# More slots for gathered rows while the mixers run, and four PSUM banks by turns for the dense U tiles

## The chip, the cores and the metric

The kernel runs on one core of a Trainium2 chip. A time is the device time of one execution in microseconds (us). The core has four engines that compute, each with its own queue of instructions in a fixed order: TensorE (PE, matmuls), VectorE (DVE), ScalarE (ACT) and GpSimd (POOL). SyncE (SP) only issues DMAs, and ACT and POOL issue DMAs too. Lower is better.

## The reference

One layer on 512 tokens of width 1024: three token mixers, merged by gates, then a mixture of 16384 one-neuron experts, from which each token takes 16 for each of 8 heads.

```python
h = rmsnorm(x, norm1_g)
z = h @ w_in                       # q, k, v and gates of the three mixers
merged = g0 * (fox(z) @ w_fox_o) + g1 * (window(z) @ w_swa_o) + g2 * (memory(z, mem) @ w_mem_o)
x = x + merged @ w_out

h = rmsnorm(x, norm2_g)
q = h @ w_q                        # 8 heads x 2 halves x 128
s1, s2 = q[..0..] @ keys1, q[..1..] @ keys2
v1, i1 = top_k(s1, 16); v2, i2 = top_k(s2, 16)
cand = v1[:, None] + v2[None, :]   # 256 a head
sv, si = top_k(cand, 16)
experts = i1[si // 16] * 128 + i2[si % 16]
a = einsum('cd,ced->ce', h, u[experts])
act = gelu(a) * softmax(sv)
x = x + einsum('ce,ced->cd', act, v[experts])
```

So a token needs 128 rows of u and 128 rows of v, 1024 numbers each.

## The kernel before

The 512 tokens are four blocks of 128. Two ways of computing the experts are mixed. Blocks 0 and 1 go by **rows**: for each of the 128 chosen experts POOL issues an indirect DMA that fetches one row of u (later of v) for each of the 128 tokens, a tile of 128x1024 (L876); DVE multiplies it with the tokens and sums (L891, for u), or adds it, scaled, to the result (L898 in the mixers, L904 later, for v). That makes 512 rows. A few are done by POOL and ACT instead ("apart"). Blocks 2 and 3 go **dense**: U tile k (128 experts) is multiplied with all 256 tokens, then weighted by a matrix of gates that is zero where an expert was not chosen, and the product with V tile k is summed over all 128 k.

The order of the work:

- `mixers(0)` for block 0, then the search and choice of its experts beside the begin of `mixers(1)` for blocks 1 to 3.
- `mixers(1)`: matmuls on PE in three terms of split operands (L145 to L147), with weights loaded by SP (L113, tile `raw`), cast by ACT (L119) and split by DVE (L131). Beside it the generator `beside()` does the rows of block 0, one `step()` at a time, at a priority `LATER` below the mixers; so a row fills what the mixers leave of DVE. `EARLY_ROWS` rows are done by the end of the mixers. (`fox` is one of the mixers; `fox(1, 1)` its second half of heads for blocks 1 to 3.)
- The search of blocks 1 to 3: PE multiplies with w_pq (L113 loads) and with the keys (`keys`, loaded at L744, used at L760), ACT copies the scores (L763), DVE finds the best (L717 to L721). One row is done per `PER_ROW` of the search's cost. The first `FIRST_U` = 4 dense U tiles lie here.
- The cover: from here DVE, POOL and PE keep the order in which the code is written. PE does `COVER` dense U tiles one after the other (L1040, 8 matmuls in the program; ACT's gelu at L1042 empties the PSUM bank), while DVE chooses the experts and does a row per `AMONG`. The softmax's `ex` (L790) is ACT's, and waits for DVE (L814).
- The spreading: 64 steps build the gate matrices (DVE L1100 and L1118, ACT L1103 and L1121, PE L1115), with the remaining `DURING` U tiles up to `LAG` between the steps' matmuls on PE, and rows on DVE.
- The main loop over the 128 V tiles: V tile k, the U tiles that are left (split in two, L1027 and L1029) and the remaining rows, evenly spread.

A row lies in one of five buffers of tag `row` (`ROWS_IN`), and `step()` issues gathers up to `AHEAD` = 4 rows ahead of the one that it finishes. The U tiles in PSUM use the two banks of tag `mm`; the spreading's matmuls use the two of tag `sc`. The two buffers of tag `v`, and one, named `ownlo` after the change, belong to the mixers: `ownlo` holds the low half of block 0's normalised tokens, `v` the values that `fox` reads.

What sets the order in the mixers and the search is a scheduler: it places instructions by priority and by its own estimate of times. From the cover on it is the code.

Of the kernel before, what the change touches and what calls it, by code (L numbers as in the profile page):

```python
# [1 line left out]

# [24 lines left out]
DENSE = (2, 3)  # L27
ND = len(DENSE)
TD = 128 * ND
FIRST_U, COVER, DURING, AFTER = 4, 28, 25, 0  # L30
PRE_U = 13
KEPT = FIRST_U + COVER
SPILT = (128 - KEPT) // 3
AMONG, UNWEIGHED = 1.0, 14
LAG = FIRST_U + COVER + DURING + AFTER
# [15 lines left out]
UNREAD = 36  # L51
LATER = 400
PACE = {"search": 20.0, "choose": 8.0, "rows": 3.5}
EARLY_ROWS, PER_ROW, APART, NO_APART = 176, 3.4, 4, 94.0


@with_exitstack
def tile_block(ctx: ExitStack, tc: tile.TileContext, t: dict, out: bass.AP):
# [188 lines left out]
    for hf in range(2):  # L247
        squares(xg[:, 0, hf * 512:(hf + 1) * 512], xsum[:, 0, hf:hf + 1])
    nc.sync.dma_start(cst[:, 1:], t["c_mats"][:, 1:])
    hT = [chunks(by_k(x)) for x in (ep.tile([128, D], F32R, tag="own", name="own"),  # L250
                                    pp.tile([128, D], F32R, name="ownlo", bufs=1))]
    norm_t([xg[:, 0]], xsum, g1, *hT, tags=("tp", "sc", "tp", "sc", "tg", "acc", "mm", "tp"))

    identb = consts.tile([128, 128], BF16, name="identb")
# [374 lines left out]
    def mixers(g, hT):  # L629

        nb = len(GROUPS[g])
        skvf(g, hT)
        oT = new_oT(g)
        qT = fox_qkv(g, 0, hT)
        if g == 0:
            memory()
            biases()
        fox(g, 0, qT, oT)
        qT = fox_qkv(g, 1, hT)
        fox(g, 1, qT, oT)  # L640
        merged = wide(f"mg{g}", nb)
        gs = gates(g, 0, hT)
        qT = window_q(g, hT)
        branch(g, 0, merged, oT, gs)
        oT = new_oT(g)
        window(g, qT, oT)
        gs = gates(g, 1, hT)
        qT = memory_q(g, hT)
        branch(g, 1, merged, oT, gs)
        oT = new_oT(g)  # L650
        recall(g, qT, oT)
        gs = gates(g, 2, hT)
        if g == 0:
            get_x()
        branch(g, 2, merged, oT, gs)

        mT = [by_k(ep.tile([128, D], F32, tag="own", name="own"))] if nb == 1 else pair(nb)
        if nb == 1:
            for q in range(2):
                ps = bank("tp")  # L660
                for i in range(4):
                    PE.transpose(ps[:, i * 128:(i + 1) * 128], merged[:, (4 * q + i) * 128:(4 * q + i + 1) * 128], ident)
                ps, dst = ps.rearrange("p (k s) -> p k s", k=4), slice(4 * q, 4 * q + 4)
                A.activation(mT[0][:, dst], ps, AF.Copy, scale=0.5)
        else:
            for ct, src in enumerate(chunks(by_k(merged))):
                A.activation(mT[0][:, ct], src, AF.Copy, scale=0.5)
                V.scalar_tensor_tensor(mT[1][:, ct], src, 0.5, mT[0][:, ct].bitcast(F32),  # L668
                                       op0=OP.mult, op1=OP.subtract)
        mT = [chunks(x) for x in mT]  # L670
        x1, sums = by_token(wide(f"mg{g}", nb)), new_sums(4)
        for c in range(4):
            xs = [new_g(256) for _ in range(nb)]
            cols = slice(c * 256, c * 256 + 256)
            for lb, b in enumerate(GROUPS[g]):
                nc.sync.dma_start(xs[lb], t["x"][b * 128:(b + 1) * 128, cols])

            def use(b, ps):
                V.tensor_add(x1[:, b, cols], xs[b], ps)
                squares(x1[:, b, cols], sums[:, b, c:c + 1])  # L680

            if nb == 1:
                gemm_plain(mT[0], t["w_out"][c], 256, use, load_raw)
            else:
                gemm_nat(mT, t["w_out"][c], 256, nb, use)
        return x1, sums
# [173 lines left out]


    JOBS = [(b, tab, j) for b in (0, 1) for tab in "uv" for j in range(NJ)]
    known, issued, done, ahead, flying, rpool = [2 * NJ], [0], [0], [AHEAD], {}, []
    begun_v = set()

    def step(apart=False):

        while issued[0] < min(known[0], done[0] + ahead[0] + 1):
            n = issued[0]
            issued[0] += 1  # L870
            b, tab, j = JOBS[n]
            if ahead[0] > AHEAD and n % (ROWS_IN + MORE) >= ROWS_IN:
                r = wp.tile([128, WSLOT], F32, tag="raw", name="row")[:, :D]
            else:
                r = rpool[0].tile([128, D], F32, tag="row", name="row", bufs=ROWS_IN)
            G.indirect_dma_start(out=r, out_offset=None, in_=t["peer_" + tab],  # L876
                                 in_offset=bass.IndirectOffsetOnAxis(ap=eidx[b][:, j:j + 1], axis=0))
            flying[n] = r
        n = done[0]
        done[0] += 1  # L880
        b, tab, j = JOBS[n]
        r, c = flying.pop(n), slice(j, j + 1)
        if tab == "u" and b and j == 0:
            A.copy(two[0], h2n[b])
        if tab == "u" and apart:
# [26 lines left out]
    def beside():  # L912
# [25 lines left out]
        pace[0], share[0] = "rows", 0.0  # L938
        credit[0] += 20.0
        rpool.append(ctx.enter_context(tc.tile_pool(name="rows", bufs=1, side="right")))  # L940
        while done[0] < EARLY_ROWS:
            step()
            yield 1.4
# [24 lines left out]
    next(side[0])  # L968
    share[0] = 0.5
    xb, sums = mixers(1, hT)  # L970
    side[0] = iter(())
    mixing.close()
    two.append(ctx.enter_context(tc.tile_pool(name="two", bufs=1, space=bass.MemoryType.PSUM)).tile([128, D], F32, name="two"))
    for lb, b in enumerate(GROUPS[1]):
# [42 lines left out]
    def dense_u(k):  # L1017
# [17 lines left out]
            return  # L1035
        w = w.rearrange("p (n w) -> p n w", n=KC)
        yield
        ps = bank("mm")
        for dc in range(KC):
            PE.matmul(ps[:, :TD], w[:, dc], h2f[dc], start=dc == 0, stop=dc == KC - 1)  # L1040
            yield
# [328 lines left out]
```

## Time and profile before

| | us |
|---|---|
| runs of the kernel, three | 1571.1, 1570.54, 1567.91 (median 1570.54) |
| the profiled execution, its own time | 1565.71 |
| its span in the trace | 1563.9 |
| busy: PE, DVE, ACT, POOL | 1499.1, 1420.1, 812.0, 779.5 |
| granted clock of PE, mean | 0.991 |
| moved by DMA | 533.48 MB, 341 GB/s over the span |

The profiled execution is one run; its rows give durations and waits. An engine's idle time has a releaser, the event that came last before it went on. A row in a timeline reads: start, busy us, engine, line, operation, output and inputs, count, and in brackets the idle time before it with its releaser. The chain of work that ended last, followed back, has these shares of the span by engine:

```profile
PE 46%; issue 17%; POOL 13%; DVE 12%; DMA 8%; ACT 4%; POOLq 0%; another core or an unknown queue 0%; SPq 0%; DVEq 0%; ACTq 0%
```

### The profile page before, as it was taken

Reading aid. Unit: us, or ns where it says so; the run is one execution under the profiler, and the core shown is the slowest. Engines: PE = TensorE matmul, PEld = TensorE weight load, DVE = VectorE, ACT = ScalarE, POOL = GpSimd, SP = SyncE. Lnnn points to the kernel's source line nnn. Section 1 sums busy time; section 2 is a strip of 40 time slices with the busy share of each in tenths; the row PEclk is TensorE's granted clock in tenths of the full one; section 3 lists DMA queues with packets and bytes.
Section 4 is the critical chain, followed back from the end, with each engine's and each line's share of the span. In section 5 each row is a group of like instructions: output and inputs, shape, how many; then the busy total and the mean of one; then the engine's idle time right before and its main releaser. Section 6 shows DMA issues by size and latency. Waiting matters only on the chain.

```text
span 1563.9 us, 27116 instructions
## 1 busy us (share of the span) xinstructions
PE 1499.1 (96%) x9411; PEld 1359.7 (87%) x9411; DVE 1420.1 (91%) x2675; ACT 812.0 (52%) x1804; POOL 779.5 (50%) x642
## 2 busy tenths in 40 slices
PE   8999899999998989999999999899999999999998
PEld 7999898997997988899788888788888888888887
DVE  6689387888998999899999998899999999999998
ACT  7778246646445434342117989544454544444443
POOL 1101016767566557786454665555554545545451
PEclk9999999999998999999999999999999999999999
DMA  8688647898998899876998999999999999999995
GB/s 334 227 280 297 241 161 266 321 362 294 333 360 299 301 339 347 312 288 239 327 389 286 388 399 383 365 407 404 403 411 410 404 410 406 406 411 410 410 409 211
DMA packets 180125, 533.48 MB, mean 341 GB/s; under 512 B 17660, under 2 KB 48148, under 8 KB 179988
## 3 DMA queue, kind: packets, MB, share of 16 engines
q0 software_dynamic: 73728, 268.47, 45.5%
q1 hardware_dynamic: 96180, 227.54, 39.9%
q10 hardware_dynamic: 10080, 35.75, 5.7%
q8 instruction: 74, 1.21, 0.3%
q14 instruction: 63, 0.52, 0.1%
HBM read 516.99 MB, written 14.69 MB: 340 GB/s over the span
## 4 chain that ended last, share of the span: by engine, by line
PE 46%; issue 17%; POOL 13%; DVE 12%; DMA 8%; ACT 4%; POOLq 0%; another core or an unknown queue 0%; SPq 0%; DVEq 0%; ACTq 0%
POOL row L876 12%; PE mm L1040 9%; PE mm L146 7%; PE mm L145 7%; PE mm L147 7%; DMA row<-in_peer_v_dram,eidx 3%; DMA row<-in_peer_u_dram,eidx 3%; PE sc L1115 3%; DVE two L904 2%; PE mm L752 2%; DVE wlo L131 1%; PE sc L498 1%; PE tp L376 1%; ACT whi L119 1%; DVE tmp L719 1%
## 5 line engine op out<-in xcount | busy, mean ns | idle before, releaser
L876 POOL DMA_INDIRECT row<-in_peer_v_dram,eidx x256 | 322.1, 1258 | 287.0 <-DVE two L904 162.1
L876 POOL DMA_INDIRECT row<-in_peer_u_dram,eidx x256 | 316.1, 1235 | 237.8 <-DVE scr L891 127.5
L131 DVE TENSOR_TENSOR wlo<-raw,whi 128x1024 fp32r<-128x1024 f32 (+1 forms) x228 | 277.7, 1221 | 20.1 <-ACT whi L119 17.3
L904 DVE SCALAR_TENSOR_TENSOR two<-row,acts,two 128x1024 f32<-128x1024 f32 x196 | 251.6, 1284 | 2.5 <-DMA row<-in_peer_v_dram,eidx 0.2
L119 ACT CAST whi<-raw 128x1024 fp32r<-128x1024 f32 x146 | 152.3, 1049 | 106.8 <-PE mm L146 51.1
L891 DVE SCALAR_TENSOR_TENSOR scr<-row,own 128x1024 bf16<-128x1024 f32 x128 | 156.4, 1222 | 21.2 <-DMA row<-in_peer_u_dram,eidx 20.5
L891 DVE SCALAR_TENSOR_TENSOR scr<-row,two 128x1024 bf16<-128x1024 f32 x117 | 142.2, 1215 | 7.3 <-DMA row<-in_peer_u_dram,eidx 6.3
L1168 ACT CAST ah<-ga 128x256 fp32r<-128x256 f32 x116 | 47.1, 407 | 160.9 <-PE tp L146 131.5
L203 POOL TENSOR_TENSOR rsy<-rsv,mhalf 128x4 f32<-128x4 f32 (+5 forms) x25 | 38.6, 1547 | 175.5 <-DVE rsv L202 174.6
L145 PE MATMUL mm<-hhi,whi 128*128 128x384 f32 x320 | 109.4, 342 | 2.0 <-ACT hhi L237 1.2
L146 PE MATMUL mm<-hlo,whi 128*128 128x384 f32 x320 | 109.5, 342 | 1.5 <-DVE hlo L239 1.5
L147 PE MATMUL mm<-hhi,wlo 128*128 128x384 f32 x320 | 109.4, 342 | 0.0
L1170 ACT CAST whi<-raw 128x1024 fp32r<-128x1024 f32 x96 | 100.2, 1047 | 15.4 <-DMA raw<-in_peer_v_dram 11.3
L146 PE MATMUL sc<-wlo,ah 128*128 128x512 f32 x256 | 100.9, 394 | 5.3 <-DVE wlo L131 4.1
L145 PE MATMUL mm<-whi,hhi 128*128 128x256 f32 (+1 forms) x360 | 102.8, 288 | 2.9 <-DVE g L610 1.9
L146 PE MATMUL mm<-wlo,hhi 128*128 128x256 f32 (+1 forms) x360 | 101.9, 284 | 2.1 <-DVE wlo L131 2.1
L147 PE MATMUL mm<-whi,hlo 128*128 128x256 f32 (+1 forms) x360 | 101.1, 283 | 0.8 <-DVE hlo L668 0.8
L147 PE MATMUL sc<-whi,al 128*128 128x512 f32 x256 | 101.1, 395 | 0.0
L145 PE MATMUL sc<-whi,ah 128*128 128x512 f32 x256 | 100.9, 394 | 0.0
L145 PE MATMUL tp<-whi,ah 128*128 128x512 f32 x256 | 100.7, 393 | 0.0
L146 PE MATMUL tp<-wlo,ah 128*128 128x512 f32 x256 | 100.5, 393 | 0.0
L147 PE MATMUL tp<-whi,al 128*128 128x512 f32 x256 | 100.3, 392 | 0.0
(325 smaller groups left out, 4480.0 us busy)
## 6 DMA issues: line engine op xcount, KB each, us to landing
raw<-in_peer_v_dram SPq DMA_DIRECT2D x96, 512.0 KB
hhi<-in_uT_dram ACTq DMA_DIRECT2D x68, 512.0 KB
raw<-in_w_tr_dram SPq DMA_DIRECT2D x48, 512.0 KB
raw<-in_w_nat_dram SPq DMA_DIRECT2D x40, 512.0 KB
last<-in_peer_v_dram SPq DMA_DIRECT2D x32, 512.0 KB
hhi<-in_uT_dram SPq DMA_DIRECT2D x26, 512.0 KB
raw<-in_w_o_dram SPq DMA_DIRECT2D x24, 512.0 KB
gd<-st SPq DMA_DIRECT2D x24, 512.0 KB
```

Of the source, the lines that this page charges most:

```text
L119: (cast or A.copy)(hi[:, :n * w], raw[:, :n * w])
L131: V.tensor_sub(lo, raw, hi.bitcast(F32))
L145: PE.matmul(ps, lh, rh, start=first, stop=False)
L146: PE.matmul(ps, lh, rl, start=False, stop=False)
L147: PE.matmul(ps, ll, rh, start=False, stop=last)
L876: G.indirect_dma_start(out=r, out_offset=None, in_=t["peer_" + tab], in_offset=bass.IndirectOffsetOnAxis(ap=eidx[b][:, j:j + 1], axis=0))
L891: V.scalar_tensor_tensor(scr, r, 1.0, two[0] if b else h2n[b], op0=OP.mult, op1=OP.mult, accum_out=acts[b][:, c]))
L904: V.scalar_tensor_tensor(two[0], r, acts[b][:, c], two[0], op0=OP.mult, op1=OP.add))
L1040: PE.matmul(ps[:, :TD], w[:, dc], h2f[dc], start=dc == 0, stop=dc == KC - 1)
L1115: PE.matmul(ps[:, u], o[:, 1, u], o[:, 0, u], start=True, stop=True)
L1168: A.copy(ah, a)
L1170: A.copy(hi, raw)
```

## The change

Rows get their buffers from a queue of free slots. It holds the five `row` buffers and `ownlo` from the start of the rows, and two `v` buffers from the point in `mixers(1)` at which `fox(1, 1)` has been written. While the mixers run, `step()` issues a gather whenever a slot is free, and not by a count of rows ahead; the gathers are kept in the order of the rows on POOL. Rows from number 184 on use only `row` buffers, and after the mixers the old rule holds again. `EARLY_ROWS` goes from 176 to 184, `PER_ROW` from 3.4 to 3.7. `COVER` goes from 28 to 30 and `DURING` from 25 to 23, with `KEPT` held at 32, and the U tiles k = 4 to 33 take the PSUM banks `mm`, `mm`, `sc`, `sc` by turns.

```diff
-FIRST_U, COVER, DURING, AFTER = 4, 28, 25, 0
+FIRST_U, COVER, DURING, AFTER = 4, 30, 23, 0
-KEPT = FIRST_U + COVER
+KEPT = 32
-EARLY_ROWS, PER_ROW, APART, NO_APART = 176, 3.4, 4, 94.0
+EARLY_ROWS, PER_ROW, APART, NO_APART = 184, 3.7, 4, 94.0
...
-                                    pp.tile([128, D], F32R, name="ownlo", bufs=1))]
+                                    pp.tile([128, D], F32R, tag="ownlo", name="ownlo", bufs=1))]
...
         fox(g, 1, qT, oT)
+        if g:
+            free.extend(["v"] * 2)
...
+    pre_open = [True]
+    free, held, gathers = deque(), {}, []
+
+    def borrowed(n):
+        if n >= EARLY_ROWS and "row" in free:
+            free.remove("row")
+            held[n] = "row"
+        elif n < EARLY_ROWS and free:
+            held[n] = free.popleft()
+        return held.get(n)
+
+    def slot(n):
+        tag = held.get(n, "row")
+        if tag == "row":
+            return rpool[0].tile([128, D], F32, tag="row", name="row", bufs=ROWS_IN)
+        return pp.tile([128, D], F32, tag=tag, name="row", **({"bufs": 1} if tag == "ownlo" else {}))
...
-        while issued[0] < min(known[0], done[0] + ahead[0] + 1):
+        while issued[0] < known[0] and (borrowed(issued[0]) if pre_open[0] else issued[0] <= done[0] + ahead[0]):
...
-                r = rpool[0].tile([128, D], F32, tag="row", name="row", bufs=ROWS_IN)
-            G.indirect_dma_start(out=r, out_offset=None, in_=t["peer_" + tab],
+                r = slot(n)
+            ins = G.indirect_dma_start(out=r, out_offset=None, in_=t["peer_" + tab],
...
+            if pre_open[0] and n:
+                tc.add_manual_dep(ins.ins, gathers[-1], mybir.DependencyInfo(
+                    mybir.DependencyClass.NoSync, mybir.DependencyReason.DATA), reason="rows in order")
+            gathers.append(ins.ins.name)
...
+        if pre_open[0]:
+            free.append(held.pop(n))
...
+        free.extend(["row"] * ROWS_IN + ["ownlo"])
         while done[0] < EARLY_ROWS:
...
-    side[0] = iter(())
+    side[0], pre_open[0] = iter(()), False
+    held.clear()
...
-        ps = bank("mm")
+        ps = bank("sc" if FIRST_U <= k < FIRST_U + COVER and k % 4 > 1 else "mm")
```

Line numbers shift behind the edits: L876 is L897 in the changed kernel, L898 is L925, L717 is L720, L744 is L747, L1040 is L1069, L1055 is L1084.

Three places in the order of instructions are worth seeing, each before and then changed.

On **DVE**, the end of the mixers: the rows `L898` of block 0, the splits of the search's operand (L239), the copy of `rstd` and the first `MAX` of the search. Before:

```order
L898 SCALAR_TENSOR_TENSOR mg_2281<-row,acts_213,mg_2281 128x1024
L239 SCALAR_TENSOR_TENSOR hlo<-sc,gcol,hhi 128x384
L1055 COPY rstd<-rsy 128x3
L717 MAX v_7876<-s 128x8 x3
L718 MAX_INDEX ids_7581<-v_7876,s 128x8
```

Changed:

```order
L240 SCALAR_TENSOR_TENSOR hlo<-sc,gcol,hhi 128x384
L925 SCALAR_TENSOR_TENSOR mg_2281<-row,acts_213,mg_2281 128x1024
L1084 COPY rstd<-rsy 128x3
L925 SCALAR_TENSOR_TENSOR mg_2281<-row,acts_213,mg_2281 128x1024 x3
L720 MAX v_7900<-s 128x8 x3
L721 MAX_INDEX ids_7605<-v_7900,s 128x8
```

At the copy 176 rows are done before, and 181 in the changed kernel; three more stand between it and the first `MAX`.

On **SP**, the loads at the same place, with what each waits for (DMAHW and DMASW are transfers of a queue, Pool, DVE and PE the engines): w_pq's weights, the keys, the first U tiles (`ga`, which is a buffer that they borrow). Before:

```order
L113 DMA raw<-in_w_pq_dram 128x1024 [waits DMAHW6_49,DMAHW2_49,DVE_49]
L113 DMA raw<-in_w_pq_dram 128x1024 [waits DMAHW3_49,DMAHW0_49,Pool_49]
L744 DMA keys<-in_keysT_dram 128x256 [waits DMAHW7_49,DMAHW5_49,DVE_49]
L744 DMA keys<-in_keysT_dram 128x256
L113 DMA raw<-in_w_pq_dram 128x1024 [waits DMAHW1_49,Pool_49]
L113 DMA raw<-in_w_pq_dram 128x1024 [waits DMAHW2_49,Pool_49]
L995 DMA ga<-in_uT_dram 128x1024 x2
```

Changed:

```order
L114 DMA raw<-in_w_pq_dram 128x1024 [waits DMAHW6_49,DMAHW2_49,DVE_49]
L114 DMA raw<-in_w_pq_dram 128x1024 [waits DMAHW3_49,DMAHW0_49,Pool_49]
L114 DMA raw<-in_w_pq_dram 128x1024 [waits DMAHW1_49,Pool_49]
L114 DMA raw<-in_w_pq_dram 128x1024 [waits DMAHW5_49,DMAHW2_49,Pool_49]
L747 DMA keys<-in_keysT_dram 128x256 [waits DMASW3_49,DMASW5_49,DMASW1_49,DMASW7_49,DMASW0_49,DMAHW7_49,DVE_49,PE_49]
L747 DMA keys<-in_keysT_dram 128x256
L1024 DMA ga<-in_uT_dram 128x1024 x2
```

The keys stand behind two more weight loads, and their first load waits for gathers (DMASW) and PE too, since its buffer overlies the borrowed ones; its wait for DVE is one for the first of the three rows behind the copy. On PE, 22 matmuls with w_pq stand ahead of the first with the keys that stood behind it.

On **PE**, the cover: the dense U tiles, eight matmuls each (from `ga`, `hhi` and `hlo`, buffers in which the U tiles lie). Before:

```order
L1040 MATMUL mm<-h2f,ga 128x256 x80
L1040 MATMUL mm<-h2f,hhi 128x256 x24
L1040 MATMUL mm<-h2f,hlo 128x256 x24
L1040 MATMUL mm<-h2f,hhi 128x256 x24
L1040 MATMUL mm<-h2f,hlo 128x256 x24
```

Changed:

```order
L1069 MATMUL mm<-h2f,ga 128x256 x24
L1069 MATMUL sc<-h2f,ga 128x256 x16
L1069 MATMUL mm<-h2f,ga 128x256 x16
L1069 MATMUL sc<-h2f,ga 128x256 x16
L1069 MATMUL mm<-h2f,ga 128x256 x8
L1069 MATMUL mm<-h2f,hhi 128x256 x8
L1069 MATMUL sc<-h2f,hhi 128x256 x16
```

The tiles are the same and in the same order; every second pair now goes to the banks `sc`. On ACT the three `ex` (L790) stand behind the eighth gelu before, and behind the seventh in the changed kernel.

More of the change, by code (lines that the diff above doesn't have):

```diff
@@ L1 @@
+from collections import deque
 from contextlib import ExitStack
```

## The prediction

> **What bounds the kernel now.** I first read busy time by stage, because a mean over the span hides which engine is full where. The columns are the stretch in us, its length, then busy us and instruction count of PE, PEld, DVE, ACT and POOL, the granted clock, the DMA share and GB/s.
>
> ```profile
> 242.00:508.00 266.00, 256.62 (x1716) 232.92 (x1715) 235.97 (x442) 142.64 (x358) 179.24 (x135) 0.97 0.91 326
> 508.00:636.00 128.00, 118.04 (x785) 114.04 (x784) 122.74 (x149) 51.91 (x96) 79.79 (x56) 1.00 0.92 327
> 636.00:748.00 112.00, 108.17 (x624) 103.50 (x624) 105.18 (x611) 43.98 (x75) 79.49 (x80) 1.00 0.78 280
> 748.00:828.00 80.00, 78.25 (x355) 68.33 (x355) 78.00 (x118) 9.87 (x26) 40.26 (x38) 0.98 0.97 363
> 828.00:984.00 156.00, 149.28 (x923) 135.59 (x924) 141.29 (x208) 138.24 (x512) 91.27 (x74) 0.99 0.98 357
> 984.00:1546.00 562.00, 549.10 (x3176) 480.26 (x3175) 549.66 (x651) 266.69 (x391) 281.44 (x209) 1.00 1.02 403
> ```
>
> The stages are the second mixers (242 to 636, cut in two), the search (to 748), the cover (to 828), the spreading (to 984) and the main loop (to 1546). PE is full at 92 to 98% everywhere, but nowhere alone: DVE stands at 96% before 636, 97% in the cover and 98% in the main loop, and the DMA engines are full from 748 on. So no stage has one bound, and a microsecond taken from one engine will rarely be a microsecond of time. POOL, which issues the gathers, is below 72% in all of them.
>
> Next, what one row costs and where DVE waits for rows: first the wait in 242 to 508 (total, times, longest), then the row products' groups (busy us, mean ns) of 508 to 636 and of the main loop, with the read of the sum that follows each U row, and the gathers' queue over the whole span (packets, MB).
>
> ```profile
> DVE scr L891 <- DMA row<-in_peer_u_dram,eidx: 20.5, 19, 3.3
> ...
> L898 DVE SCALAR_TENSOR_TENSOR mg<-row,acts,mg 128x1024 f32<-128x1024 f32 x48 | 66.2, 1379 | 1.9 <-DMA row<-in_peer_v_dram,eidx 1.4
> ...
> L891 DVE SCALAR_TENSOR_TENSOR scr<-row,two 128x1024 bf16<-128x1024 f32 x85 | 103.5, 1217 | 7.3 <-DMA row<-in_peer_u_dram,eidx 6.3
> L891 DVE DVE_READ_ACCUMULATOR scr<-row,two 128x1 f32 x85 | 7.0, 83 | 0.0
> ...
> q0 software_dynamic: 73728, 268.47, 45.5%
> ```
>
> A U row is 1.217 + 0.083 = 1.30 us of DVE, a V row 1.38 us. The 512 rows move 268.47 MB, so one is 0.524 MB.
>
> **The change, part by part.** The rows' places, counted in the order of the instructions: 184 instead of 176 by the end of the mixers, 25 instead of 26 in the search, 37 and 60 as before in the cover and the spreading, and so 206 instead of 213 in the main loop. Dense U tiles: 30 instead of 28 in the cover, 24 instead of 26 in the spreading.
>
> *Mixers, 242 to 636.* Three more buffers let 8 gathers fly instead of 5, so the 20.5 us for which DVE waited for rows should mostly go. The first DVE listing shows that five of the eight added rows fall before the copy of rstd, and three behind it. The five cost DVE 5 x 1.38 = 6.9 us. DVE then has slack for them, 20.5 against 6.9, but PE is 96% busy up to 508 and gains little. The ends are +6.9 (the cost in full, no wait recovered) and -8 (PE's idle time of 508 to 636 is 10.0 us, and most of it goes). I take -1.0, near zero, since PE's own busy time does not change. Gathers are only issued earlier on POOL, which has 48 us idle in 508 to 636, and move the same bytes.
>
> The other three rows come after the copy. What stands there before (DVE, SP's queue and ACT's none):
>
> ```profile
> 636.17 0.17 DVE L1055 COPY rstd<-rsy 128x3 f32<-128x3 f32 x1 [1.22 <-POOL rsy L203]
> 640.84 0.68 DVE L717 MAX8 v<-s 128x8 f32<-128x128 f32 x3 [4.50 <-ACT s L763]
> ...
> 623.80 0.80 SPq L744 DMA_DIRECT2D keys<-in_keysT_dram  x2
> ```
>
> DVE idles 4.50 us there, and 3 x 1.38 = 4.1 us fit in. But the same edit moves the load of the keys on SP behind two more weight loads and gives it a wait on DVE, for the product of the first of those three rows, because the keys' buffer overlies the borrowed ones. It will be issued near 638 to 639 instead of 623.80. Behind it on SP wait U loads that nothing needs before the next tiles; PE has 22 more weight matmuls ahead of its first keys matmul, so it does not stand still. I put DVE's start of the search 2.7 us later, less 1.4 for the row that the search has no more: DVE is 1.5 late at the cover, PE not at all. The ends of that are 0 and 4.1.
>
> *Search and cover.* Two tiles more on PE. What a tile takes, and the stall that the four banks are for, stand in ACT's and PE's timelines:
>
> ```profile
> 744.73 1.28 ACT L790 ACT_TABLE_LOAD   x1 [5.78 <-DVE sh L814]
> 746.03 0.98 ACT L790 ACTIVATE ex<-ex,rstd 128x128 f32<-128x128 f32 x3
> 747.03 1.28 ACT L1042 ACT_TABLE_LOAD   x1
> 748.33 0.66 ACT L1042 ACTIVATE ga<-mm 128x256 f32<-128x256 f32 x2
> 754.21 0.38 ACT L1042 ACTIVATE ga<-mm 128x256 f32<-128x256 f32 x1 [5.22 <-PE mm L1040]
> 757.66 0.38 ACT L1042 ACTIVATE ga<-mm 128x256 f32<-128x256 f32 x1 [3.07 <-PE mm L1040]
> 761.11 0.38 ACT L1042 ACTIVATE ga<-mm 128x256 f32<-128x256 f32 x1 [3.07 <-PE mm L1040]
> ...
> 748.76 6.49 PE L1040 MATMUL mm<-h2f,ga 128*128 128x256 f32 x21 [3.32 <-ACT ga L1042]
> ...
> 749.00:753.00 4.00, 4.00 (x12) 3.24 (x12) 3.56 (x6) 0.00 (x0) 2.97 (x3) 0.59 0.92 307
> 753.00:757.00 4.00, 4.00 (x19) 3.47 (x19) 3.96 (x4) 0.38 (x1) 2.72 (x3) 0.98 0.94 334
> ```
>
> A tile is 757.66 - 754.21 = 3.45 us, so two more are +6.9. ACT's queue is in order: the gelu that frees a bank stands behind ex, which waits for DVE. PE stops 3.32 us, and then the clock is 0.59 for some four microseconds: the tile that ends with the gelu at 754.21 began at 748.76 and took 5.4 us, 2.0 more than the rest. The stall costs 3.3 + 1.8 to 2.0, say 5.1. With four banks PE can run one tile further before it needs the gelu behind ex (it has one gelu less ahead of ex, and two banks more): 3.45 us more cover for a chain that is 1.5 us later. I expect a rest of 1.2 us, too short to lower the clock: 5.1 - 1.2 = 3.9 recovered, sum +3.0. Ends: 0 (DVE's chain not late, and its 78.00 busy of 80 still just fits) and +6.9 (nothing recovered). The two U loads that move with the tiles are 1.05 MB, 2.9 us at 363 GB/s, about what the cover grows by.
>
> The Trainium skill, "TensorE: Matmul & The Clock Gate", section "What's actually happening", says that PE's clock is halved after an idle window of some 3.4 us and comes back after about 3.4 us of work; the trace agrees (3.32 us idle, then 0.59 over four us). By it the stall costs 5.1 or, once below the window, only its own length; the sum above takes the rows alone. The same page's section "A second HAM failure mode: psum-queue depth-cycling" speaks against the change: PE working through PSUM banks by turns may idle between groups and keep falling to half clock. Here tiles already alternate over two banks at a steady 3.45 us and full clock, so I give it little.
>
> *Spreading.* Two tiles fewer on PE: -6.9. It waits there for ACT and DVE, which wait for it in turn:
>
> ```profile
> DVE ga L1118 <- PE sc L1115: 11.8, 12, 2.1
> ...
> PE sc L1115 <- ACT st L1121: 4.0, 5, 1.4
> ```
>
> DVE is 91% and ACT 89% busy over 156 us; over 149 us they would be 95 and 93%. So not all of it comes: -5.5, with the ends -7 (PE alone) and -3 (ACT and DVE set the pace).
>
> *Main loop.* Seven U rows fewer: DVE -7 x 1.30 = -9.1; DMA -3.67 MB at 403 GB/s = -9.1. PE is not relieved; its idle time there is 562 - 549.1 = 12.9 us, of which it waits for DVE
>
> ```profile
> PE mm L147 <- DVE ulo L1029: 5.0, 6, 1.6
> PE mm L147 <- DVE u L1029: 4.7, 7, 1.1
> PE sc L146 <- DVE wlo L131: 2.0, 3, 0.9
> ```
>
> 11.7 us by these. DVE and DMA both give 9.1, PE would then have to lose nearly all its waits: I take -7.0, ends -9.1 and -3 (a quarter of PE's waits).
>
> Sum: -1.0 + 3.0 - 5.5 - 7.0 = **-10.5 us**. Against the profiled execution (1565.71, a span of 1563.9 and 1.8 around it) that is 1555.2. The median of the runs is 1570.54, 4.8 us longer (0.3%), and what I predict is such a median: 1570.5 - 10.5 = **1560.0**.
>
> **The rivals.**
>
> *The mixers take the rows at full price.* For it: DVE is 96% busy in 508 to 636, where the last rows are, and waits little for V rows (1.4 us in the L898 group). Against it: the waits of 242 to 508 lie earlier, so that rows can move forward. +6.9 in place of -1.0: 1568.
>
> *The main loop is PE's.* For it: PE 98% busy. Against it: DVE and DMA just as full. -3 there: 1564. If instead the stall stays as it is (the added banks do nothing), the cover is +6.9 and the time is 1564 too.
>
> *The mixers gain.* If the 20.5 us of waits held PE up, through products that came late in DVE's order, the stretch loses 8 us: 1553. For it: PE's idle time of 10 us in 508 to 636, most of it behind DVE or ACT; against it: up to 508 PE waits for almost nothing.
>
> *Slower: gathers hold up the weights.* Eight in flight instead of five share the DMA engines, at 0.91 busy, with the loads of the mixers' weights.
>
> ```profile
> L119 ACT CAST whi<-raw 128x1024 fp32r<-128x1024 f32 x40 | 41.9, 1048 | 55.8 <-PE mm L146 39.6 <-issue 9.1 <-PE mm L147 7.0
> ...
> 633.14 0.34 PE L145 MATMUL mm<-hhi,whi 128*128 128x384 f32 x1
> 633.32 0.34 PE L146 MATMUL mm<-hlo,whi 128*128 128x384 f32 x1
> ```
>
> This is the cast of the 40 weight tiles between 376 and 636. Three gathers more are 1.57 MB, 4.8 us at 327 GB/s. A tile is 24 matmuls at 0.18 us, 4.3 us; from where a load comes over two tiles, 8.6 us, later than it is now wanted, PE stops. If one load in eight does so by the 4.8 us, that is 5 x 4.8 = +24: 1584. Against it: the casts never wait for a load in that row, only for PE to free their buffers, so the loads are early now; and the waits on slots keep the bytes the same.
>
> *Slower: the banks cost clock* (the page's rule above): were half of the 30 tiles of the cover at 5.4 instead of 3.45 us, +29: 1589.
>
> **How the numbers follow.** Forecast 0.45 (1553 to 1567), main loop PE's 0.12, stall stays 0.06, mixers gain 0.10, rows at full price 0.13, late weights 0.11, banks cost clock 0.03. A measurement tells 0.2% from no change, 3.1 us: faster is below 1567.4, slower above 1573.7. Faster holds the forecast, the two at 1564, the gain, and a little of the full price: 0.74. Same holds the rest of that: 0.12. Slower holds the last two: 0.14. The terms' best ends together give -24, their worst +8; the range leaves these corners and the 0.14 out and reaches from 1550 to 1572.
>
> **What would show it.** The mixers: the waits of DVE for U rows in 242 to 508 fall from 20.5 us to below 8, and the copy of rstd stands within 3 us of 636. Search: the first MAX8 near 643.5, PE's first tile of the cover no later than now. Cover: no stall of PE above 1.5 us near 749, the clock full there, and its end near 831. Spreading 150 to 152 us long, main loop 554 to 556. It is wrong if casts wait for raw loads in the mixers, if DVE reaches the search over 5 us later, or if the main loop keeps its 562 with PE's idle time grown to nothing and DVE's to over 20 us.

## The result, and the profile after

| | before | changed |
|---|---|---|
| runs | 7 | 7 |
| median, us | 1570.31 | 1560.85 |
| lowest and highest, us | 1565.45, 1571.81 | 1559.41, 1564.3 |
| profiled execution, own time, us | 1565.71 | 1560.02 |

The ratio is 0.9941, with a 95% interval of 0.9928 to 0.9955: 7 to 11 us faster. The forecast was 1560.0. The sum came out right, but two of its five terms did not, and the eight rows, to which the forecast gave most of the gain, turn out to be an even trade. So the nearness of the number is partly luck, as the runs below show.

First the stages of the changed kernel, by the same windows as before (length; busy us and count of PE, PEld, DVE, ACT, POOL; clock; DMA share; GB/s):

```profile
242.00:508.00 266.00, 258.44 (x1755) 236.01 (x1755) 243.81 (x460) 146.87 (x374) 188.70 (x141) 0.98 0.92 337
508.00:636.00 128.00, 114.96 (x754) 110.47 (x753) 124.30 (x143) 51.01 (x95) 74.95 (x54) 0.97 0.89 324
636.00:748.00 112.00, 110.91 (x647) 106.85 (x646) 105.68 (x604) 41.09 (x70) 82.73 (x81) 1.00 0.78 278
748.00:828.00 80.00, 80.00 (x372) 70.44 (x371) 78.25 (x127) 12.94 (x30) 39.92 (x38) 1.00 0.97 365
828.00:984.00 156.00, 147.65 (x910) 132.77 (x909) 143.28 (x215) 136.76 (x509) 90.66 (x74) 0.99 0.99 363
984.00:1546.00 562.00, 553.69 (x3199) 485.04 (x3198) 548.46 (x646) 270.62 (x400) 275.65 (x203) 1.00 1.01 398
```

PE fills the cover now, 80.00 of 80 at full clock, where it had 78.25. But in 508 to 636 it does *less* than before, 114.96 against 118.04, at a clock of 0.97 against 1.00. Something is lost there.

Fixed windows cut two kernels at different work, so these two rows are only a hint. To compare stages I take five events that both have: the cast of the 70th weight tile, that of the 131st, the gelu of the second dense U tile, and the first and the last matmul of the spreading. Before:

```profile
228.81 1.04 ACT L119 CAST whi<-raw 128x1024 fp32r<-128x1024 f32 x1
...
613.39 1.06 ACT L119 CAST whi<-raw 128x1024 fp32r<-128x1024 f32 x1 [0.37 <-PE mm L147]
...
707.45 0.38 ACT L1042 ACTIVATE ga<-mm 128x256 f32<-128x256 f32 x1 [2.98 <-PE mm L1040]
...
830.33 1.32 PE L1115 MATMUL sc<-o 128*128 128x128 f32 x8 [3.31 <-issue]
...
981.98 1.05 PE L1115 MATMUL sc<-o 128*128 128x128 f32 x8
```

Changed:

```profile
233.28 1.05 ACT L120 CAST whi<-raw 128x1024 fp32r<-128x1024 f32 x1
...
614.45 1.06 ACT L120 CAST whi<-raw 128x1024 fp32r<-128x1024 f32 x1 [0.38 <-PE mm L148]
...
712.31 0.38 ACT L1071 ACTIVATE ga<-mm 128x256 f32<-128x256 f32 x1 [2.98 <-PE mm L1069]
...
835.91 1.39 PE L1144 MATMUL sc<-o 128*128 128x128 f32 x6 [2.40 <-ACT o L1132]
...
984.74 1.05 PE L1144 MATMUL sc<-o 128*128 128x128 f32 x8
```

The lengths between them (the last matmul of the spreading ends 1.05 after the start shown; the rest of the span is the main loop), with those of every other kernel that was traced later, worked out in the same way, and the times against the kernel before:

| kernel | start | mixers | head | cover | spreading | main | ratio to before |
|---|---|---|---|---|---|---|---|
| before | 228.8 | 384.6 | 94.1 | 122.9 | 152.7 | 580.9 | 1 |
| changed | 233.3 | 381.2 | 97.9 | 123.6 | 149.9 | 572.4 | 0.9941 (0.9928 to 0.9955) |
| changed, again | 235.0 | 382.3 | 98.8 | 123.6 | 151.3 | 572.4 | 0.9935 (0.9915 to 0.9954) |
| rows_only | 232.4 | 384.2 | 98.9 | 126.0 | 150.7 | 573.1 | 0.9987 (0.9968 to 1.0005) |
| slots_176 | 228.3 | 382.6 | 90.0 | 122.3 | 152.7 | 581.6 | 0.9978 (0.9961 to 0.9995) |
| rows184_five | 232.2 | 387.9 | 98.9 | 130.0 | 152.3 | 573.6 | 1.0029 (1.0014 to 1.0044) |
| tiles_only | 232.3 | 383.0 | 94.4 | 123.6 | 147.5 | 579.7 | 0.9977 (0.9956 to 0.9998) |
| tiles_two_banks | 230.2 | 385.7 | 94.1 | 127.1 | 149.4 | 581.3 | 1.0023 (1.0008 to 1.0038) |
| banks_only | 232.9 | 385.3 | 94.1 | 122.4 | 150.6 | 581.8 | 1.0018 (1.0004 to 1.0033) |
| rows_banks | 228.9 | 384.2 | 98.8 | 122.1 | 151.0 | 573.5 | 0.9957 (0.9942 to 0.9971) |
| no_rows | 233.8 | 384.3 | 90.0 | 123.6 | 148.3 | 580.9 | 0.9950 (0.9931 to 0.9968) |
| keys_8 | 229.5 | 382.3 | 96.6 | 123.6 | 150.1 | 572.7 | 0.9953 (0.9936 to 0.9969) |
| pool3_after | 231.3 | 382.8 | 94.7 | 123.7 | 150.4 | 575.0 | 0.9928 (0.9905 to 0.9951) |
| pool3_k8 | 230.9 | 384.3 | 94.0 | 125.5 | 149.0 | 572.6 | 0.9954 (0.9938 to 0.9969) |

The column "start" is a warning: all these programs do the same work in the same order on PE, DVE and ACT up to that point, and yet one trace needs 228.3 and another 235.0. A difference of two traces holds up to 7 us of that. The stages are steadier: the head is 94.1 to 94.4 in four kernels that share its code, the main loop 579.7 to 581.8 in six; the mixers (383.0 to 385.7 in four with one code) and the spreading (2 us and more) are not so steady, and only their means are used.

The waits that the prediction named, in the changed kernel: DVE for U rows in 242 to 508 (total, times, longest), and then PE's waits in the main loop.

```profile
DVE scr L918 <- DMA row<-in_peer_u_dram,eidx: 6.0, 2, 3.5
```

```profile
PE sc L147 <- DVE wlo L132: 3.5, 3, 2.2
PE mm L148 <- DVE u L1058: 2.9, 6, 0.9
PE mm L148 <- DVE ulo L1058: 1.7, 3, 0.9
```

20.5 us went to 6.0, and PE's waits for DVE from 11.7 to 8.1. ACT's timeline at the place of the old stall:

```profile
749.03 1.28 ACT L793 ACT_TABLE_LOAD   x1 [8.66 <-DVE sh L817]
750.32 0.99 ACT L793 ACTIVATE ex<-ex,rstd 128x128 f32<-128x128 f32 x3
751.33 1.28 ACT L1071 ACT_TABLE_LOAD   x1
752.62 0.38 ACT L1071 ACTIVATE ga<-sc 128x256 f32<-128x256 f32 x1
752.90 0.65 ACT L1071 ACTIVATE ga<-mm 128x256 f32<-128x256 f32 x2
753.80 0.38 ACT L1071 ACTIVATE ga<-sc 128x256 f32<-128x256 f32 x1 [0.24 <-PE sc L1069]
757.25 0.38 ACT L1071 ACTIVATE ga<-sc 128x256 f32<-128x256 f32 x1 [3.07 <-issue]
```

ACT waits even longer for DVE (8.66 us). Then it empties three banks that PE has filled meanwhile, and the fourth 0.24 us later. PE shows no wait there at all.

### The profile page after: what moved, and what is told of

Same layout as the page of the kernel before. It is cut to its first block, busy times and chain, and to the rows that moved or that the text cites. A ratio compares the mean times of both kernels' runs of the same rounds, so it can differ in the third digit from the quotient of the medians.

```text
span 1558.2 us, 27098 instructions
## 1 busy us (share of the span) xinstructions
PE 1500.2 (96%) x9411; PEld 1362.7 (87%) x9411; DVE 1421.3 (91%) x2673; ACT 812.2 (52%) x1806; POOL 779.7 (50%) x642
## 4 chain that ended last, share of the span: by engine, by line
PE 47%; issue 17%; POOL 11%; DMA 11%; DVE 10%; ACT 4%; POOLq 0%; DVEq 0%; SPq 0%; ACTq 0%
POOL row L897 10%; PE mm L147 8%; PE mm L146 8%; PE mm L148 8%; PE mm L1069 7%; DMA row<-in_peer_u_dram,eidx 4%; DMA row<-in_peer_v_dram,eidx 4%; PE sc L1069 3%; DVE wlo L132 3%; PE sc L1144 2%; DVE two L931 2%; PE mm L755 2%; DVE scr L918 1%; DVE o L1129 1%; PE tp L377 1%
## 5 line engine op out<-in xcount | busy, mean ns | idle before, releaser
L897 POOL DMA_INDIRECT row<-in_peer_v_dram,eidx x256 | 324.1, 1266 | 300.1 <-DVE two L931 173.4
L897 POOL DMA_INDIRECT row<-in_peer_u_dram,eidx x256 | 314.7, 1229 | 220.4 <-DVE scr L918 116.0
L931 DVE SCALAR_TENSOR_TENSOR two<-row,acts,two 128x1024 f32<-128x1024 f32 x190 | 244.0, 1284 | 3.0 <-DMA row<-in_peer_v_dram,eidx 0.8
L1197 ACT CAST ah<-ga 128x256 fp32r<-128x256 f32 x116 | 47.1, 407 | 151.7 <-PE tp L147 124.8
```

The source lines that it names most:

```text
L897: ins = G.indirect_dma_start(out=r, out_offset=None, in_=t["peer_" + tab], in_offset=bass.IndirectOffsetOnAxis(ap=eidx[b][:, j:j + 1], axi ...
L931: V.scalar_tensor_tensor(two[0], r, acts[b][:, c], two[0], op0=OP.mult, op1=OP.add))
L1197: A.copy(ah, a)
```

## What was lost at the end of the mixers

The head, from the 131st cast to the second gelu, is 3.8 us longer. DVE reaches the search late, in place of 636.17 for the copy of `rstd` and 640.84 for the first MAX8:

```profile
638.84 0.16 DVE L1084 COPY rstd<-rsy 128x3 f32<-128x3 f32 x1
...
648.65 0.68 DVE L720 MAX8 v<-s 128x8 f32<-128x128 f32 x3 [5.76 <-ACT s L766]
```

DVE, POOL and PE between 624 and 633, each from its own timeline:

```profile
624.75 0.61 DVE L240 SCALAR_TENSOR_TENSOR hlo<-tp,gcol,hhi 128x384 fp32r<-128x384 f32 x1
625.27 5.83 DVE L925 SCALAR_TENSOR_TENSOR mg<-row,acts,mg 128x1024 f32<-128x1024 f32 x1
631.02 0.60 DVE L240 SCALAR_TENSOR_TENSOR hlo<-sc,gcol,hhi 128x384 fp32r<-128x384 f32 x1
```

```profile
624.30 1.01 POOL L897 DMA_INDIRECT row<-in_peer_v_dram,eidx  x1 [0.30 <-issue]
625.33 4.68 POOL L130 TENSOR_TENSOR wlo<-raw,whi 128x1024 fp32r<-128x1024 f32 x2
```

```profile
628.09 0.52 PE L146 MATMUL mm<-hhi,whi 128*128 128x384 f32 x1
631.77 0.87 PE L235 MATMUL sc<-cst,mg 128*128 128x128 f32 x3 [3.17 <-DVE hlo L240]
```

One row product, 1.28 us elsewhere, shows 5.83. It is not waiting in DVE's queue: it has started. It begins with two weight splits that POOL does back to back (4.68 us), and ends 1.1 us behind them. Behind it on DVE stands a split that PE needs; PE stands 3.17 us. In the windows around it the clock (third column from the end) is halved:

```profile
630.00:632.00 2.00, 0.23 (x1) 0.26 (x2) 2.00 (x3) 0.00 (x0) 0.01 (x1) 0.50 0.79 221
632.00:634.00 2.00, 2.00 (x8) 2.00 (x8) 2.00 (x5) 0.58 (x1) 0.00 (x0) 0.50 0.54 197
```

The clock was already 0.50 from 628 to 630, before most of this wait: PE was busy for only 0.96 us of 626 to 628. Not all of the half clock is therefore owed to the 3.17 us.

Before, the splits on POOL stood apart and no product took more than 3.3 us. The Trainium skill, "SBUF — State Buffer", section "SBUF: two separate sides", says that VectorE with two inputs from SBUF and GpSimd share a pair of ports that one of them holds for a whole instruction; that would give nearly this, and 5.83 against 4.68 + 1.28 = 5.96 agrees. In one thing the trace differs: that section of the Trainium skill gives the ports to whichever starts first, but here the product, recorded 0.06 us before the first split, is the one that waits, and through both splits. That the product is held by POOL's splits is what the runs show: in all fourteen traces no product of this form (`mg<-row,acts,mg`) over 1.5 us stands without a split on POOL beside it, and pool3_after below takes the splits away. That the ports are the reason rests on the Trainium skill alone.

## The experiments

In each, the edit is against the kernel named; the numbers asked for are in the table above.

**rows_only**, against the changed kernel:

```diff
-FIRST_U, COVER, DURING, AFTER = 4, 30, 23, 0
+FIRST_U, COVER, DURING, AFTER = 4, 28, 25, 0
...
-        ps = bank("sc" if FIRST_U <= k < FIRST_U + COVER and k % 4 > 1 else "mm")
+        ps = bank("mm")
```

> The rows' half of the change alone: borrowed slots, 184 rows by the end of the mixers and 3.7 per row in the search, with 28 tiles in the cover, two banks. Theory A (the halves add up, and the rows carry most of it): the mixers gain 3 to 4 us, their end gives them back, the main loop loses 7 to 8.5 us with its 7 rows: 1570 - 8 = about 1562, and the stall near 750 stays at 3 us or more. Rival B (the main loop is PE's, its rows are nearly free): about 1567, and the fall must come from the tiles.

Measured 1567.1 against 1568.3, a ratio of 0.9987 that reaches from 0.9968 to 1.0005: 2 us or nothing, not 8. The main loop did lose 7.8. But the head is 4.8 longer, and the stall is larger than before, PE's one wait in 700 to 800 being

```profile
PE mm L1069 <- ACT ga L1071: 5.9, 1, 5.9
```

So A's main loop and stall were right and its sum was not; B's number was right for another reason. Alone, the rows give back most or all of what they save.

**tiles_only**, against the kernel before:

```diff
-FIRST_U, COVER, DURING, AFTER = 4, 28, 25, 0
+FIRST_U, COVER, DURING, AFTER = 4, 30, 23, 0
-KEPT = FIRST_U + COVER
+KEPT = 32
...
-        ps = bank("mm")
+        ps = bank("sc" if FIRST_U <= k < FIRST_U + COVER and k % 4 > 1 else "mm")
```

> The tiles' half alone: 30 tiles in the cover, 24 less 1 in the spreading as in the change, four banks by turns; rows, their slots and their places as before. Theory A: the cover grows by 6.9 less the stall of 5.1, so +1.8 or a little less, the spreading loses 3 to 5.5: -1 to -4, about 1568. Rival B: the tiles carry most of the change, about 1563. The stall of PE near 749 should be gone, and the half clock after it, by both.

**tiles_two_banks**: the same with `bank("mm")` for all tiles.

> As the tiles' half, but all tiles in the two banks of tag mm as before. If the four banks are what removes the stall, it stays at 3 us and the time is 4 to 5 us above the tiles' half, near 1572 to 1574, no faster than before. If the banks do nothing and only the moved tiles count, it equals the tiles' half within 1.5 us.

The tiles' half is 3.6 us faster by its ratio, 0.9977 (0.9956 to 0.9998), within theory A's -1 to -4. Its median, 1563.4, is the number that B gave, but beside a kernel before of 1568.3 on that chip; the interval, 0.3 to 6.9 us, hardly leaves out B's 7. With two banks the ratio is 1.0023, slower than before, though at 1570.6 a little below the range expected. The cover differs by 3.5 us (127.1 against 123.6). With two banks PE's wait of 3.3 us is there again, and with four there is none:

```profile
PE mm L1040 <- ACT ga L1042: 3.3, 1, 3.3
```

The banks remove the stall. (The half clock did not come with it this time: 748 to 760 of the trace with two banks has a granted clock of 1.00.)

**banks_only** is tiles_only with 28 and 25; **rows_banks** is the changed kernel with 28 and 25.

> The kernel before with the four banks alone: 28 tiles in the cover, 25 less 1 in the spreading, rows as before. Theory F (the banks carry the tiles' half; moving two tiles from the spreading to the cover adds 6.0 us there and takes 2.5 to 5 off there): the stall is gone, the stretch from the second gelu to that of tile 31 is 5.3 us shorter as in the tiles' half, the spreading as long as before, time 1564 to 1566, as fast as the tiles' half within 2 us or faster. Rival G (the moved tiles carry it): 2 us or more slower than the tiles' half, 1567 or above.

> The changed kernel with 28 tiles in the cover instead of 30: rows' half and banks. Theory F: rows make DVE late at the cover (the stall cost 4.1 us more in the rows' half than before), and the banks hide that too; so rows and banks together give mixers and head +1 to +2, cover -5.3, main loop -8: 1557 to 1560, as fast as the full change or up to 2 us faster. Rival G (two tiles more in the cover are needed, since the spreading has no room): 1562 to 1565.

Both stalls went, as F said, and in banks_only the stretch from the second gelu to that of tile 31 became 5.3 us shorter than before. But banks_only is no faster than before (1.0018): G's number. Its PE timeline at the start of the spreading shows why:

```profile
824.77 1.46 PE L1040 MATMUL sc<-h2f,hhi 128*128 128x256 f32 x6
826.07 0.38 PE L1087 MATMUL tp<-cst,e 128*128 128x128 f32 x2
826.29 0.27 PE L1087 MATMUL tp<-cst,gate 128*128 128x128 f32 x1
834.65 2.05 PE L1115 MATMUL sc<-o 128*128 128x128 f32 x8 [8.09 <-ACT o L1103]
```

PE is done early and stands 8.09 us, because DVE and ACT set when the spreading can begin. In the changed kernel, with 30 tiles, that wait is 2.40 us. So the two tiles moved into the cover cost it 1.5 us or less (rows_banks 122.1 against 123.6, banks_only 122.4 against 123.6), not 6.9: they run in time that the banks had set free. Neither half of this edit gains alone in the kernel with the old rows. With the rows in, it is otherwise: rows_banks came out at 1561.4, ratio 0.9957, between F and G. That is 0.003 below rows_only (0.9987), so there the banks gain alone: the rows had made the stall larger. It is not told apart from the full change, so the two moved tiles are not shown to add anything there.

**slots_176** (the kernel before with the borrowed slots alone) and **rows184_five** (184 rows and 3.7 with the five old slots), as edits of rows_only and of the kernel before:

```diff
-EARLY_ROWS, PER_ROW, APART, NO_APART = 184, 3.7, 4, 94.0
+EARLY_ROWS, PER_ROW, APART, NO_APART = 176, 3.4, 4, 94.0
```

```diff
-EARLY_ROWS, PER_ROW, APART, NO_APART = 176, 3.4, 4, 94.0
+EARLY_ROWS, PER_ROW, APART, NO_APART = 184, 3.7, 4, 94.0
```

> The kernel before with the borrowed slots alone: eight in place of five, but 176 rows by the end of the mixers, 3.4 per row in the search, 28 tiles, two banks. Theory A (the slots take DVE's waits for U rows away, and PE gains what it waited for DVE): the waits of 20.5 us fall below 8, the mixers are 3 us shorter or more, and the time falls by up to 3 us unless their end gives it back. Rival B (PE sets the mixers' pace, the waits cost nothing): the waits fall just as far, and the mixers' length stays within 1.5 us.

> The kernel before with 184 rows by the end of the mixers and 3.7 per row in the search, but the old five slots. Theory A (the borrowed slots pay for the eight rows): the rows cost DVE 6 to 7 us in the mixers, which come out 2 to 5 us longer than with the slots, and the main loop still loses 7 to 8.5 us. Rival B (DVE has room for the rows as it stands): the mixers are as long as with the slots, within 1.5 us, and the borrowed slots do nothing but delay the keys; then this is as fast as the rows' half or faster, 1564 to 1567.

The slots alone are faster, 0.9978 (0.9961 to 0.9995); the rows without them are slower, 1.0029. DVE's waits for U rows in 242 to 508 were 6.6 and 17.1 us, and the mixers with the slots 382.6, some 2 us less than the mean of 384.7 for the old rows. That lies between A and B, and one trace of a stage that scatters by 2.7 us can't decide between them. With five slots the eight rows make mixers, head and cover 3.3, 4.8 and 7.1 us longer; A holds. With the slots alone the head is 4.1 us *shorter* than before, which neither theory had. The trace suggests why: with rows that come sooner the last of the 176 is done before 620, and of the products beside POOL's splits one of 2.7 us is left, where there were three; PE has no wait above 1.2 us from 612 to 650.

**no_rows**: the changed kernel with 176 and 3.4.

> The changed kernel with its slots, its 30 tiles and its four banks, but 176 rows by the end of the mixers and 3.7 back to 3.4 in the search. Theory H (the eight rows pay in the mixers and the head of the search what they save in the main loop; the slots and the banks carry the change): head of the search some 8 us shorter than in the change, main loop 8 us longer, time equal to the change within 2 us, 1559 to 1562. Rival I (the rows' 8 us in the main loop are the gain, as the forecast had it): 1565 to 1568.

H: 1561.4, ratio 0.9950, not told apart from the change. The head is 7.9 us shorter, the main loop 8.5 longer. The eight rows are an even trade, as far as intervals of some 3 us can tell. Slots and tiles as halves of this kernel agree with it: 0.9978 x 0.9977 is 0.9955.

**keys_8**, against the changed kernel:

```diff
-        if n >= EARLY_ROWS and "row" in free:
+        if n >= EARLY_ROWS - 8 and "row" in free:
...
-        elif n < EARLY_ROWS and free:
+        elif n < EARLY_ROWS - 8 and free:
```

**pool3_after**, against the changed kernel, and **pool3_k8** with both:

```diff
-    k_u, share[0] = 0, 1.0
+    k_u, share[0], due[0] = 0, 1.0, -3.0
```

> The changed kernel, but its last eight rows before the search use only row buffers and leave the borrowed ones, so that the keys' load waits for an older row and stands before the two weight loads again; the two weight splits that POOL did back to back near 625 then stand apart. Theory C: in the profile of the changed kernel one row product of DVE took 5.8 us beside these two splits, PE stood 3 to 4 us and went to half clock, and this cost some 4 us at the start of the search; here no row product there is over 3.5 us, PE reaches the first keys matmul near 640 instead of 647, and the time falls by 2.5 to 4 us to 1557 to 1558. Rival D: DVE, not PE, sets the end of the cover, and gives nothing back: 1560 to 1562, with PE idle before the spreading.

> The changed kernel, but the first three weight splits of w_pq are done by DVE and not by POOL; order of the loads as in the change. Theory C (DVE's row product took 5.8 us because POOL did two splits beside it): no row product there is over 1.5 us, PE has no stall over 1.5 us between 620 and 640 and keeps its clock, the head of the search shortens by 2 to 4 us though DVE does 3.7 us of splits more; time 1557 to 1560. Rival E (the product waited for its row's data, or the delay is the keys' load): a product of over 4 us stays, the head is as long as in the change or longer by the splits, 1560 to 1564.

> The changed kernel with both edits to the head of the search: its last eight rows leave the borrowed slots, and the first three splits of w_pq are DVE's. If the late keys and the splits beside DVE's products are two losses, each of 1 to 3 us, the head is below 96 us and the time 1555 to 1558, below both. If they are one and the same, it equals the kernel with the three splits moved within 1.5 us.

With the keys loaded early (622.18 in place of 640.32) the first matmul with them starts at 639.37 as expected, but the head is only 1.2 to 2.2 us shorter: products of 3.53 and 4.07 us are left, each over one split on POOL, so the bound of 3.5 that C set was missed, and the time, 1559.7, lies between C and D. Its ratio, 0.9953, is no better than that of the change. With the three splits on DVE the keys are still late (637.09) and no product before the copy of rstd is long:

```profile
627.33 1.22 DVE L132 TENSOR_TENSOR wlo<-raw,whi 128x1024 fp32r<-128x1024 f32 x1
628.47 1.28 DVE L925 SCALAR_TENSOR_TENSOR mg<-row,acts,mg 128x1024 f32<-128x1024 f32 x1
...
631.31 1.27 DVE L925 SCALAR_TENSOR_TENSOR mg<-row,acts,mg 128x1024 f32<-128x1024 f32 x1
...
633.11 2.59 DVE L925 SCALAR_TENSOR_TENSOR mg<-row,acts,mg 128x1024 f32<-128x1024 f32 x2
```

The head falls to 94.7, 3.1 to 4.1 us off, though DVE does three splits more; behind the copy one product of 3.3 us is left. PE has one wait of 1.9 us, a little over what C allowed, and does not keep its clock as C said (0.60 from 638 to 640, 0.55 to 642). With both edits the head is 94.0, but the time is 1559.8, above what two separate losses would give. That is 1.0 from pool3_after by the medians, which are of two chips; by the ratios, 0.9954 and 0.9928, they are further apart, with intervals that overlap, so the times settle nothing here. By the length of the head, the splits on POOL beside the products are most of the loss against the kernel before, and the keys add little to it. What it is worth in time stays open: pool3_after is 1558.8 (0.9928) beside 1560.5 (0.9935) for the changed kernel on the same chip, no difference that this can tell, and none of these kernels is shown to beat the change. pool3_k8 shows one thing that takes part of it back: PE is early again, and a stall of 1.7 us returns near 730, in the cover.

**after_again**

> The changed kernel once more, unaltered, beside the other three: its time against before gives the base for them, expected 1560 to 1562 at a ratio of 0.994; and a second trace of it shows what of the differences between two traces is chance. The stretch up to 229 us, where both programs are the same, was 4.5 us longer in the first trace of it than in the trace of before; by chance alone it should now lie anywhere between 228 and 234 us, and the 5.8 us product should be there again.

The time and the 5.8 us product (5.82) came again, and so did the head (98.8 after 97.9) and the main loop (572.4 both times); "start" was 235.0, above the range that I gave.

## Why the prediction was right, step by step

In this table the measured value is a difference of means over the traces that share the code of that stage.

| step | forecast | measured |
|---|---|---|
| mixers | -1.0 (-8 to +6.9) | -1.7 (four traces each, 381.2 to 385.7) |
| their end, on PE | 0 | +4.4 (98.6 against 94.2, four each) |
| cover | +3.0 (0 to +6.9) | +0.7 (one pair) |
| spreading | -5.5 (-7 to -3) | -2.2 (149.5 with 30 tiles, eight traces; 151.7 with 28, six) |
| main loop | -7.0 (-9.1 to -3) | -7.9 (573.2, eight traces; 581.0, six) |
| sum | -10.5 | -6.7; by the medians -9.5 |

*Mixers.* As forecast: the waits went (20.5 to 6.0), and PE hardly gained by it. Without the slots, in rows184_five, the rows made the mixers 3.3 us longer than before; that is the side of the rival that charged them in full, at half of its 6.9. My line that DVE stands at 96% before 636 was true for 508 to 636 alone; in 242 to 508 its row says 235.97 of 266 us, 89%.

*Their end.* This step failed. I wrote that DVE would be 1.5 us late and "PE not at all", and looked at the keys' load. DVE's first MAX8 came at 648.65 in place of 640.84 (and of the 643.5 forecast), and PE's head was 3.8 to 4.8 us longer. "DVE reaches the search over 5 us later" was one of the signs by which the forecast would be wrong, and it came true, also when both are counted from the 131st cast (34.2 us against 27.5). The order that I had shown for SP was the sign, read too narrowly: two weight loads ahead of the keys also mean two splits on POOL without a gather between them, and the durations of 2.5 to 3.3 us of row products beside single splits were in the trace of before. Against no_rows the eight rows cost the head some 8 us; moving three splits gives back 3.1 to 4.1 of them.

*Cover.* The forecast let PE's tiles set its end and asked for +6.9 - 3.9. The recovery was larger (5.3 up to tile 31), since PE came 4.9 us late to it itself; where PE comes earlier, in pool3_k8, a rest of 1.7 us is there (the forecast expected 1.2). And DVE and ACT set the end, so two tiles more came nearly free. The trace of before had the sign of it: PE waited 3.31 us ahead of the spreading with 28 tiles already, which the forecast's sum for the cover has no term for. The rival "the stall stays" fell with tiles_only; the rule on bank cycling had no effect here, the clock of the cover is 1.00.

*Spreading.* Mis-sized: two tiles fewer bring 2.2 by the means, less than the end of -3; single traces scatter by 2 to 4 us. Over that window DVE's waits for PE fell from 11.8 to 8.0, PE's for ACT rose from 4.0 to 5.5, and those of its weight loads (PEld) from 6.8 to 9.8:

```profile
PEld sc L1144 <- ACT st L1150: 9.8, 11, 2.5
DVE ga L1147 <- PE sc L1144: 8.0, 8, 2.3
...
PE sc L1144 <- ACT st L1150: 5.5, 4, 2.1
```

So PE waits more for ACT's copies where it had tiles to do, as the end of -3 in that step supposed. The traces of tiles_only and after_again agree (5.6 and 5.0 us of such waits with 30 tiles; 3.1 and 2.8 with 28 tiles, in banks_only and rows_banks). That ACT alone explains the rest was not tried.

*Main loop.* Right, and nearer to the full 9.1 of DVE and DMA than I took. PE's waits for DVE fell by 3.6 of these 7.9 us, and its idle time in the window from 12.9 to 8.3; where the rest comes from was not traced. But the net of the rows is about zero, since the head pays for them; the forecast had no term for that.

*The sum.* Two failures of opposite sign, the head +4.4 and the cover -2.3, and the small spreading leave -6.7 from the traces. The medians say -9.5, their interval 7 to 11. The 3 us between are within what the traces scatter, and what they are is not settled: without their start, the two traces of the changed kernel are 10.2 and 6.6 us shorter than the one of before. The forecast gave the rows' edits 8.0 us (mixers and main loop) and the tiles' 2.5. Alone, the rows brought 2 us or nothing and the tiles 3.6, and the change without its eight rows is not told apart from the change. So, as far as the runs tell, the gain comes from the slots and from the banks with their tiles, and not from the seven rows that the main loop lost. That the forecast met the size is in good part luck; of its terms only those of the mixers and the main loop are confirmed.

The rival of late weight loads fell: no cast waits for a load in 376 to 636 of the changed kernel, and the mixers did not grow. Rows and tiles as halves make 0.9987 x 0.9977 = 0.9964, the whole 0.9941. The difference, 3.6 us, is not clear of the intervals. It has the size of what the rows' larger stall costs without the banks (cover 126.0 against 122.9), which is gone with them (122.1 in rows_banks).

## What to carry to other kernels

Two edits that each gain nothing alone can gain together: in the kernel with the old rows, free banks take a stall away, and work moved into the time so freed makes something of it. A test of halves must then include their sum, and the kernel that they are tried in matters: with the new rows the banks gained without the moved work. A total that comes out as forecast does not confirm its terms; take out the term that should carry it and see. When a change moves loads in one queue, follow what the loads set off on every engine, also those that only share a port. Cut traces at events, not at times, and trace the same code twice before a few microseconds of a stage are explained.

## What was not expected of the hardware

A DVE product of 128x1024 with two operands in SBUF took 1.28 us alone. Beside one split of 128x1024 on POOL it took 2.2 to 4.1 us, and 5.8 us when POOL did two in a row; the profile counts all of it as busy. All 35 such long products of the fourteen traces end 1.08 or 1.09 us behind the end of the split. Where the split began 0.45 us or more into the product, the product took its 1.28 us (18 times, and once, in keys_8, it was held all the same).

The length of one stall does not tell what PE's clock does behind it. In the changed kernel the 2.40 us ahead of the spreading were followed by half clock, which its windows show:

```profile
837.00:839.00 2.00, 2.00 (x8) 1.73 (x8) 2.00 (x4) 2.00 (x8) 0.00 (x0) 0.50 0.74 299
```

The same wait of 2.40 us left the clock at 1.00 in tiles_only (832 to 840) and keys_8 (831 to 839), and 1.9 us in pool3_after were followed by 0.60 and 0.55. The stall of 3.32 us in the cover was followed by 0.59 in the trace of before, and by 1.00 in tiles_two_banks, where the stretch up to tile 31 was 1.7 us shorter for it (114.1 against 115.8). So a stall below the 3.4 us that the prediction names is not safe, one of 3.32 is not always punished, and the 1.8 us that the prediction added for the half clock are a chance and not a fixed price.

And the first 229 us of the same program took between 228.3 and 235.0 us in fourteen traces.
